# A fused conv/attention block: its first modulation moved to TensorE in four column groups, and a softmax scaling moved to GpSimd

## The chip, the core and the metric

The kernel runs on one core of a Trainium2 chip. A core has five engines that run side by side and wait for each other through semaphores: TensorE (PE in the profile; PEld is its weight load) does matmuls from SBUF into PSUM, VectorE (DVE), ScalarE (ACT) and GpSimd (POOL) work element by element, and SyncE (SP) here only issues DMAs. ACT issues some small DMAs too. The metric is the device time of one execution in microseconds (us); less is better.

## The reference

Two layers work on 256 latent tokens and 256 context tokens of width 1,024, in float32. Before any layer a vector `c` (and `c_ctx` for the context) gives nine modulation vectors per layer, three for each of three sublayers:

```python
mod = (jax.nn.silu(c) @ mod_w[i] + mod_b[i])          # 9 x 1024 per layer
h   = rms_norm(t, norm_g) * (1 + scale) + shift       # before each sublayer
t   = t + gate * sublayer(h)
```

The sublayers of layer 0 are a SwiGLU feed-forward network, a short convolution and another SwiGLU; those of layer 1 are a SwiGLU, an attention with 8 query heads and 2 key heads over all 512 tokens, and a SwiGLU. Only the latent tokens are the output. What matters here: nothing can be multiplied before the first shift (`B00` in the kernel) and scale (`A00`) are known, since the very first feed-forward product takes the modulated, normalised `x` of both streams.

## The kernel before

Activations are kept transposed: a tile has 128 of the 1,024 features on its partitions and 512 tokens (two streams `s` of 256) in its free dimension, so `x` is 8 tiles (`k`). To keep float32 accuracy with faster matmuls, `split` (L91) cuts every operand into a high part (ACT, L92, names ending in h) and a low part (DVE, L93, names ending in l), and `mm3` (L112) does three matmuls, wh*mh, wh*ml, wl*mh (lines L116, L117, L118). Raw weights arrive in a ring of three 1 MB buffers `wr` (L87), issued in order on SP (L88); a buffer is free again when its last reader is through.

Modulation is computed in one of two ways. A *unit* (L136, `junk`) is one DVE instruction that multiplies 1,024 columns of transposed weights with the broadcast `silu(c)` in `scbc` and sums them; `tick` sprinkles such units over the whole kernel, and `mod_ready` forces those that are due. For the first shift and scale, which everything waits for, there is `mod_pe` (L736): eight TensorE matmuls of 128x2 by 128x256 accumulate a row pair in PSUM, ACT copies it (L746), and two matmuls against `ident` turn it into columns (L748), which DVE adds to the bias (L753).

The start is written as a list of steps, issued in the program in this order:

```python
FIRST_STEPS = (
    "W0 P11 P10 P00 N0 P01 N1 P12 W1 S M00 M10 M01 M11 D02 N2 M02 D13 W2 D03 M12 M20 M21 N3 "
    "M03 M22 M13 M23"
)
```

The first digit of P and D is 0 for the shift and 1 for the scale, the last digit is the quarter `q` of the features (two `k` tiles). P is `mod_pe`, D is `mod_dve` (the same by four DVE units), N normalises and modulates a quarter (`norm_q` with `norm_k`: per tile and stream a DVE product `t`, L250, an ACT sum `hh`, L260, a DVE difference `hl`, L261, and an ACT copy for later, L265), W loads and splits one of the first three feed-forward tiles, M multiplies tile `i` with quarter `q` (12 matmuls into the PSUM pair `pg`, `pu`), and S loads and activates `scbc`. Ahead of the list, 36 matmuls of ones (L719) keep TensorE busy, and the root mean squares of both streams are found (`ss`). The list gives the program order; a planner in the framework then sets each engine's final order by priority and by when it expects operands, so an engine's instructions may stand in another order than the list. It does so for TensorE too.

All six large PSUM buffers belong to the three M tiles, so the following tile, and the stage `w13` of five more such tiles behind it, starts when the first of them is through.

In the attention, `scores` (L1022) makes for each head and each of two query halves a score tile `psc` of 128x512 on TensorE, its maximum on DVE (L1031), a negated scaled maximum (L1033), the exponential `e` with its sum on ACT (L1039), the sum's reciprocal `r` (DVE, L1043) and the scaled `pn` (DVE, L1047). `turn` (L1051) transposes `pn` on TensorE (L1056) and splits it (`pth` on ACT, `ptl` on DVE), and `mix` multiplies with the values. Scores run two heads ahead of `turn`; each head has a `tick(2)`, two more DVE units.

Of the kernel before, what the change touches and what calls it, by code (L numbers as in the profile page):

```python
# [9 lines left out]
F32 = mybir.dt.float32  # L10
F32R = mybir.dt.float32r
BF16 = mybir.dt.bfloat16
AF = mybir.ActivationFunctionType
ALU = mybir.AluOpType
AX = mybir.AxisListType

P = 128
D = 1024
KT = D // P
S = 256  # L20
# [6 lines left out]
KVH = 2  # L27
EPS = 1e-6
WARM = 36

FIRST_STEPS = (
    "W0 P11 P10 P00 N0 P01 N1 P12 W1 S M00 M10 M01 M11 D02 N2 M02 D13 W2 D03 M12 M20 M21 N3 "
    "M03 M22 M13 M23"
)


# [1 line left out]
def hybrid_kernel(ctx: ExitStack, tc: tile.TileContext, a: dict, out: bass.AP):  # L40
    nc = tc.nc
    const = ctx.enter_context(tc.tile_pool(name="const", bufs=1))
# [27 lines left out]
    ccol = cload("ccol", [P, KT, 2])  # L70
# [5 lines left out]
    ident = cload("ident", [P, P])  # L76
    ones = const.tile([P, P], F32, name="ones", tag="ones")
    nc.vector.memset(ones, 1.0)
    eps_t = const.tile([P, 1], F32, name="eps_t", tag="eps_t")
    nc.vector.memset(eps_t, EPS)  # L80
    sccol = const.tile([P, KT, 2], F32, name="sccol", tag="sccol")
    nc.scalar.activation(out=sccol, in_=ccol, func=AF.Silu)
    scbc = mp.tile([P, 2, D], F32, name="scbc", tag="scbc", bufs=1)


# [35 lines left out]
    modv = {}  # L121
# [29 lines left out]
    def mod_job(l, ch, pair):  # L151
        mod_tile(l, ch)
        raw = load_raw(a["modT"][l, ch * 4 + pair])
        for j in range(2):
            for v in range(streams(l, ch)):
                mod_unit(l, ch, pair, raw, j, v)
# [557 lines left out]
    h32 = {}  # L714
    idle = psmall("idle")


    for _ in range(WARM):
        nc.tensor.matmul(idle[:, :P], ones, ones, start=True, stop=True)  # L719
    for k in range(KT):  # L720
        square_add(k, 0, T2)
    ris = []
    for s in range(2):
        ris.append(tp.tile([P, S], F32, name=nm("ris"), tag=f"ris{s}", bufs=1))
        nc.scalar.copy(ris[s], rms_inv(s, (accs[s], accs[s, "last"])))
    A00 = const.tile([P, KT, 2], F32, name="A00", tag="A00")
# [3 lines left out]
        out=sb1, in0=modb[:, 0, KT : 2 * KT], scalar1=1.0, scalar2=None, op0=ALU.add  # L730
    )

    def both(t):
        return t.unsqueeze(2).to_broadcast([P, 2, 2])

    def mod_pe(ch, q):  # L736

        raw = load_raw(a["mod0"][ch, q])
        pr = psmall("pr")
        for k in range(KT):  # L740
            nc.tensor.matmul(
                pr[:2, :S], sccol[:, k, :], raw[:, k * S : k * S + S],
                start=(k == 0), stop=(k == KT - 1),
            )
        row = tp.tile([P, S], F32, name=nm("row"), tag="t", bufs=3)
        nc.scalar.copy(row[:2, :], pr[:2, :S])  # L746
        for j in range(2):
            nc.tensor.matmul(  # L748
                pr[:, S + 2 * j : S + 2 * j + 2], row[:2, j * P : j * P + P], ident[:2, :2],
                start=True, stop=True,  # L750
            )
        k2 = slice(2 * q, 2 * q + 2)
        nc.vector.tensor_tensor(  # L753
            out=(A00 if ch else B00)[:, k2, :],
            in0=pr[:, S : S + 4].rearrange("p (k v) -> p k v", v=2),
            in1=both(sb1[:, k2] if ch else modb[:, 0, k2]),
            op=ALU.add,
        )
# [11 lines left out]

    pps = [(psum("pg"), psum("pu")) for _ in range(3)]

    def mod_dve(ch, q):
        mod_job(0, ch, q)
        if ch:
            k2 = slice(2 * q, 2 * q + 2)
            nc.vector.tensor_scalar(
                out=A00[:, k2, :], in0=modv[0, 1][:, k2, :], scalar1=1.0, scalar2=None,
                op0=ALU.add,
            )  # L780

    ws, gs0 = {}, []

    def load_sc():
# [4 lines left out]
    def first_w(i):  # L789
# [8 lines left out]

    steps = {
        "P": mod_pe,  # L800
        "D": mod_dve,
        "S": load_sc,
        "W": first_w,
        "N": norm_q,
        "M": lambda i, q: w13_mm(pps[i], ws[i], h, range(2 * q, 2 * q + 2), 0, T2),
    }
    for step in FIRST_STEPS.split():
        steps[step[0]](*(int(c) for c in step[1:]))
    done[0, 0] = done[0, 1] = 16
    h = FirstBlocks(h, h32)  # L810
    for i in range(3):
# [15 lines left out]
    for m in range(KT):  # L827
# [4 lines left out]
        for c0, c1 in ((0, S), (S, T2)) if m == 0 else ((0, T2),):  # L832
# [13 lines left out]
        d = tp.tile([P, T2], F32, name=nm("d"), tag="gm", bufs=3)  # L846
        nc.vector.tensor_scalar(
            out=d, in0=u, scalar1=convk[:, 1, m : m + 1], scalar2=None, op0=ALU.mult
# [4 lines left out]
            out=d2[:, :, 1:], in0=u2[:, :, : S - 1], scalar=convk[:, 0, m : m + 1],  # L853
# [3 lines left out]
            out=d2[:, :, : S - 1], in0=u2[:, :, 1:], scalar=convk[:, 2, m : m + 1],  # L857
# [164 lines left out]
    def scores(hd):  # L1022
        kv = hd // (HEADS // KVH)
        r_ = []
        for qt in range(2):
            o = (hd % 2) * S + qt * P
            ps = psum("psc")
            mm3(ps, tuple(t[:, o : o + P] for t in qs[hd // 2]), ks[kv], True, True)
            ci = hd * 2 + qt
            mx = ap.tile([P, 1], F32, name=nm("mx"), tag="mx", bufs=4)  # L1030
            nc.vector.reduce_max(mx, ps, axis=AX.X)  # L1031
            nb = ap.tile([P, 1], F32, name=nm("nb"), tag="nb", bufs=4)
            nc.vector.tensor_scalar(  # L1033
                out=nb, in0=mx, scalar1=scq[:, ci : ci + 1], scalar2=-1.0,
                op0=ALU.mult, op1=ALU.mult,
            )
            e = tp.tile([P, T2], F32, name=nm("e"), tag="sg", bufs=3)
            sm = ap.tile([P, 1], F32, name=nm("sm"), tag="smx", bufs=4)
            nc.scalar.activation(  # L1039
                out=e, in_=ps, func=AF.Exp, scale=scq[:, ci : ci + 1], bias=nb, accum_out=sm  # L1040
            )
            r = ap.tile([P, 1], F32, name=nm("r"), tag="r", bufs=4)
            nc.vector.reciprocal(r, sm)  # L1043
            if qt == 0:
                pn2 = hot("pn", F32)
            pn = pn2[:, qt * T2 : qt * T2 + T2]
            nc.vector.tensor_scalar(out=pn, in0=e, scalar1=r, scalar2=None, op0=ALU.mult)  # L1047
            r_.append(pn)
        return r_

# [54 lines left out]
def _layout(inp):  # L1105
    f = lambda k: np.asarray(inp[k])
    d = {}

    def kp(w, width):

        k, n = w.shape
        v = w.reshape(k // P, P, n // width, width).transpose(2, 1, 0, 3)
        return v.reshape(n // width, P, (k // P) * width)

    tok = np.concatenate([f("x")[0], f("ctx")[0]], axis=0)
    d["xT"] = tok.T.reshape(KT, P, T2).transpose(1, 0, 2)
    d["c2"] = np.stack([f("c")[0], f("c_ctx")], axis=0)
    d["ccol"] = d["c2"].reshape(2, KT, P).transpose(2, 1, 0)
    mw = f("mod_w")
    m0 = mw[0][:, : 2 * D].reshape(KT, P, 2, 4, S)  # L1120
    d["mod0"] = m0.transpose(2, 3, 1, 0, 4).reshape(2, 4, P, 2048)
    d["modT"] = mw.transpose(0, 2, 1).reshape(2, 36, 2, P, D).transpose(0, 1, 3, 2, 4).reshape(2, 36, P, 2048)
    d["modb"] = f("mod_b").reshape(2, 72, P).transpose(2, 0, 1)
    d["normg"] = f("norm_g").reshape(2, 3, KT, P).transpose(3, 0, 1, 2)
    w13 = f("ffn_w13").reshape(2, 2, KT, P, 2, NM, P)[:, :, :, :, ::-1]
    d["w13"] = w13.transpose(0, 1, 5, 3, 4, 2, 6).reshape(2, 2, NM, P, 2048)
    w2 = f("ffn_w2").reshape(2, 2, NM, P, KT // 2, 2, P)
    w2 = w2.transpose(0, 1, 4, 3, 5, 2, 6)
# [12 lines left out]
    d["cw_b"] = kp(ci[:, :D], 256)  # L1141
    d["cw_out"] = kp(f("conv_w_out")[0], 256)
    d["convk"] = f("conv_k")[0].reshape(3, KT, P).transpose(2, 0, 1)
    wqkv = f("attn_w_qkv")[0]
    d["wq"] = kp(wqkv[:, :D], 256)
    d["wk"] = kp(wqkv[:, D : D + 256], 256)[0]
    d["wv"] = kp(wqkv[:, D + 256 :], 256)[0]
    d["wo"] = kp(f("attn_w_o")[0], 256)
    d["qg"] = f("attn_q_g")[0].reshape(P, 1)
    d["kg"] = f("attn_k_g")[0].reshape(P, 1)  # L1150


    pos = np.arange(S)
    inv = np.float32(10000.0) ** (-np.arange(32, dtype=np.float32) / np.float32(32))
    ar = (pos // 64).astype(np.float32)[:, None] * inv
    ac = (pos % 64).astype(np.float32)[:, None] * inv
    ang = np.concatenate([ar, ar, ac, ac], axis=-1).astype(np.float32)
    d["cosT"] = np.cos(ang).T
    sign = np.where(np.arange(P) % 64 < 32, -1.0, 1.0).astype(np.float32)
    d["sinT"] = np.sin(ang).T * sign[:, None]  # L1160
    d["ident"] = np.eye(P, dtype=np.float32)
    return {k: np.ascontiguousarray(v) for k, v in d.items()}


# [17 lines left out]
```

## Time and profile before

| what | value |
|---|---|
| median of three runs | 1605.62 us (1602.84 to 1607.07) |
| the profiled execution's own time | 1606.83 us |
| its span in the profile | 1605.0 us |
| TensorE clock granted, mean | 0.991 |
| first weight product of the first feed-forward network | 38.50 us after the start |
| mod0 loads (P) on SP | 5 of 1,024 KB, 7.6 us from issue to landing in the middle |
| DVE units of modulation (L136) | 236, 1,279 ns each |
| softmax scalings (L1047) | 16 on DVE |

A busy TensorE in the profile is not a TensorE at its best: a matmul with two useful columns counts as busy in the same way as one with 128. So the start is read from the names of the instructions, and the attention from what TensorE waits for.

### The profile page before, as it was taken

What the parts mean: (1) busy time and instruction counts of PE and PEld (TensorE: products, weight loads), DVE (VectorE), ACT (ScalarE), POOL (GpSimd) and SP (SyncE); (2) the same over time, 40 slices, a digit from 0 to 9 for tenths busy, and PEclk for the clock granted to TensorE, in tenths of its full rate; (3) what the DMA queues carried; (4) which work ended last, traced back from release to release, by engine and by line L of the source; (5) the groups of instructions that cost most, each with busy time, mean ns of one, the idle gap of its engine ahead of it and who ended that gap; (6) DMA issues with size and microseconds to landing.
All of it is one profiled execution on the core that took longest, in us unless ns stands there. A gap on an engine that the chain in (4) does not pass through costs nothing.

```text
span 1605.0 us, 25629 instructions
## 1 busy us (share of the span) xinstructions
PE 1578.0 (98%) x10590; PEld 1451.0 (90%) x10590; DVE 1322.5 (82%) x2021; ACT 717.7 (45%) x1100; POOL 0.2 (0%) x4
## 2 busy tenths in 40 slices
PE   9999999999999999999999999999999998899999
PEld 5788998998888899999899899889899897899999
DVE  4988788879998879799797998898797889965554
ACT  4632452544322366335255375245254455454443
POOL 0000000000000000000000000000000000000000
PEclk9999999999999999999999999999999999989999
DMA  8555334334565422452433423453433463755452
GB/s 299 184 184 184 105 101 175 105 117 159 183 223 196 158 79 90 148 184 99 153 130 122 170 78 117 159 184 99 164 120 112 165 217 107 280 191 186 169 197 106
DMA packets 38278, 248.79 MB, mean 155 GB/s; under 512 B 5136, under 2 KB 6928, under 8 KB 12304
## 3 DMA queue, kind: packets, MB, share of 16 engines
q1 hardware_dynamic: 35712, 245.38, 43.6%
q10 hardware_dynamic: 2448, 1.76, 0.4%
q8 instruction: 83, 1.36, 0.3%
q14 instruction: 35, 0.29, 0.1%
HBM read 244.77 MB, written 1.05 MB: 153 GB/s over the span
## 4 chain that ended last, share of the span: by engine, by line
PE 88%; DVE 8%; ACT 1%; DMA 1%; issue 1%; ACTq 0%; SPq 0%; DVEq 0%
PE py L117 9%; PE py L116 9%; PE py L118 9%; PE p L118 6%; PE p L117 6%; PE p L116 6%; PE q L118 5%; PE q L116 5%; PE q L117 5%; DVE junk L136 3%; PE pg L116 2%; PE pg L117 2%; PE pg L118 2%; PE pu L118 2%; PE pu L117 2%; PE pu L116 2%
## 5 line engine op out<-in xcount | busy, mean ns | idle before, releaser
L92 ACT ACTIVATE wh<-wr 128x1024 fp32r<-128x1024 f32 (+2 forms) x276 | 276.6, 1014 | 395.3 <-PE py L117 108.5
L93 DVE TENSOR_TENSOR wl<-wr,wh 128x1024 fp32r<-128x1024 f32 (+2 forms) x276 | 320.1, 1165 | 96.6 <-ACT wh L92 96.1
L136 DVE CUSTOM_DVE_ANT_0 junk<-wr,scbc,modb 128x1024 bf16<-128x1024 f32 x236 | 301.8, 1279 | 33.7 <-DMA wr<-in_modT 31.0
L116 PE MATMUL py<-gh,wh 128*128 128x512 f32 (+1 forms) x746 | 263.2, 353 | 0.0
L117 PE MATMUL py<-gl,wh 128*128 128x512 f32 (+1 forms) x746 | 263.1, 353 | 0.0
L118 PE MATMUL py<-gh,wl 128*128 128x512 f32 (+1 forms) x746 | 262.8, 352 | 0.0
L118 PEld LDWEIGHTS py<-gh,wl 128*128 128x128 f32 x746 | 141.1, 189 | 18.9
L116 PEld LDWEIGHTS py<-gh,wh 128*128 128x128 f32 x746 | 141.2, 189 | 18.6
L117 PEld LDWEIGHTS py<-gl,wh 128*128 128x128 f32 x746 | 141.2, 189 | 18.2
L93 DVE TENSOR_TENSOR wl<-ws,wh 128x1024 fp32r<-128x1024 f32 x108 | 131.7, 1223 | 29.0 <-ACT wh L92 28.9
L92 ACT ACTIVATE wh<-ws 128x1024 fp32r<-128x1024 f32 x108 | 113.5, 1058 | 68.7 <-PE p L117 35.5
L118 PE MATMUL p<-th,wl 128*128 128x256 f32 x432 | 122.3, 283 | 0.0
L117 PE MATMUL p<-tl,wh 128*128 128x256 f32 x432 | 122.2, 283 | 0.0
L116 PE MATMUL p<-th,wh 128*128 128x256 f32 x432 | 122.2, 283 | 0.0
L440 DVE SCALAR_TENSOR_TENSOR x<-py,G,x 128x256 f32<-128x256 f32 x168 | 73.9, 477 | 22.5 <-PE py L118 22.2
L116 PE MATMUL q<-bh,wh 128*128 128x256 f32 x320 | 90.6, 283 | 0.0
L117 PE MATMUL q<-bl,wh 128*128 128x256 f32 x320 | 90.6, 283 | 0.0
L118 PE MATMUL q<-bh,wl 128*128 128x256 f32 x320 | 90.6, 283 | 0.0
L116 PEld LDWEIGHTS p<-th,wh 128*128 128x128 f32 x432 | 82.9, 192 | 0.3
L117 PEld LDWEIGHTS p<-tl,wh 128*128 128x128 f32 x432 | 82.9, 192 | 0.3
L118 PEld LDWEIGHTS p<-th,wl 128*128 128x128 f32 x432 | 82.9, 192 | 0.0
L116 PE MATMUL pg<-hh,wh 128*128 128x256 f32 (+1 forms) x240 | 75.8, 316 | 4.0 <-ACT hh L260 4.0
(236 smaller groups left out, 4029.8 us busy)
## 6 DMA issues: line engine op xcount, KB each, us to landing
wr<-in_w SPq DMA_DIRECT2D x88, 1024.0 KB, 4.9
wr<-in_modT SPq DMA_DIRECT2D x67, 1024.0 KB, 4.9
wr<-in_w2b SPq DMA_DIRECT2D x32, 896.0 KB, 4.5
wr<-in_w2a SPq DMA_DIRECT2D x16, 1024.0 KB, 4.8
wr<-in_cw_cx SPq DMA_DIRECT2D x8, 1024.0 KB, 4.9
wr<-in_mod SPq DMA_DIRECT2D x5, 1024.0 KB, 7.6
wr<-in_cw_b SPq DMA_DIRECT2D x4, 1024.0 KB, 4.8
wr<-in_cw_out SPq DMA_DIRECT2D x4, 1024.0 KB, 4.8
```

The source lines that it names most:

```text
L92: nc.scalar.activation(out=hi, in_=src, func=AF.Copy)
L93: nc.vector.tensor_tensor(out=lo, in0=src, in1=hi.bitcast(F32), op=ALU.subtract)
L116: nc.tensor.matmul(ps, wh, mh, start=first, stop=False, **kw)
L117: nc.tensor.matmul(ps, wh, ml, start=False, stop=False, **kw)
L118: nc.tensor.matmul(ps, wl, mh, start=False, stop=last, **kw)
L136: nc.vector.tensor_tensor_reduce(out=junk, in0=raw[:, j * D : j * D + D], in1=scbc[:, v, :], scale=1.0, scalar=modb[:, l, col : col + 1], ...
L440: nc.vector.scalar_tensor_tensor(out=x[:, m, s * S : s * S + S], in0=ps[:, o : o + S], scalar=g[:, m, s : s + 1], in1=x[:, m, s * S : s * ...
```

## The change

- **The first modulation.** All eight quarters of shift and scale are now P steps; the D steps are gone. `sccol` is widened from 2 to 32 columns per tile, the rest zero. In a P step the eight matmuls are spread by `tile_position` over four groups of 32 columns of the array, two each, and so four partial sums land on four groups of 32 partitions in PSUM. ACT copies all 128 partitions, and the turn, a step of its own (T), multiplies with the new constant `rowsum`, which adds up the four groups while it turns.
- **The order.** The list begins with P10 and P00, has T steps, one F step (12 more matmuls of ones into `pps[2][0]`) and S at its end. `tc.manual_schedule` for TensorE makes that engine keep the order of the list; the other engines are still planned.
- **The softmax.** `pn = e * r` is issued on GpSimd instead of VectorE.

```diff
 FIRST_STEPS = (
-    "W0 P11 P10 P00 N0 P01 N1 P12 W1 S M00 M10 M01 M11 D02 N2 M02 D13 W2 D03 M12 M20 M21 N3 "
-    "M03 M22 M13 M23"
+    "P10 P00 T10 T00 F W0 N0 W1 M00 W2 M10 P11 M20 P01 T11 T01 N1 M01 P12 M11 P02 T12 T02 N2 "
+    "M21 P13 M02 P03 T13 T03 N3 M12 M22 M03 M13 M23 S"
 )
...
-    sccol = const.tile([P, KT, 2], F32, name="sccol", tag="sccol")
-    nc.scalar.activation(out=sccol, in_=ccol, func=AF.Silu)
+    sccol = const.tile([P, KT, 32], F32, name="sccol", tag="sccol")
+    nc.vector.memset(sccol, 0.0)
+    nc.scalar.activation(out=sccol[:, :, :2], in_=ccol, func=AF.Silu)
+
+    rowsum = cload("rowsum", [P, 2])
...
+    def fill(ps, n):
+
+        for _ in range(n):
+            nc.tensor.matmul(ps[:, :P], ones, ones, start=True, stop=True)
+
+    fill(idle, WARM)
...
         for k in range(KT):
+            g = 32 * (k % 4)
             nc.tensor.matmul(
-                pr[:2, :S], sccol[:, k, :], raw[:, k * S : k * S + S],
-                start=(k == 0), stop=(k == KT - 1),
+                pr[g : g + 32, :S], sccol[:, k, :], raw[:, k * S : k * S + S],
+                start=(k < 4), stop=(k >= 4), tile_position=(0, g),
             )
         row = tp.tile([P, S], F32, name=nm("row"), tag="t", bufs=3)
-        nc.scalar.copy(row[:2, :], pr[:2, :S])
+        nc.scalar.copy(row, pr[:, :S])
+        rows[ch, q] = pr, row
+
+    def mod_turn(ch, q):
+
+        pr, row = rows[ch, q]
         for j in range(2):
             nc.tensor.matmul(
-                pr[:, S + 2 * j : S + 2 * j + 2], row[:2, j * P : j * P + P], ident[:2, :2],
+                pr[:, S + 2 * j : S + 2 * j + 2], row[:, j * P : j * P + P], rowsum,
                 start=True, stop=True,
             )
...
-        "D": mod_dve,
+        "T": mod_turn,
+        "F": lambda: fill(pps[2][0], FILL),
...
-    for step in FIRST_STEPS.split():
-        steps[step[0]](*(int(c) for c in step[1:]))
+    with tc.manual_schedule(engines={mybir.EngineType.PE}):
+        for step in FIRST_STEPS.split():
+            steps[step[0]](*(int(c) for c in step[1:]))
...
-            nc.vector.tensor_scalar(out=pn, in0=e, scalar1=r, scalar2=None, op0=ALU.mult)
+            nc.gpsimd.tensor_scalar(out=pn, in0=e, scalar1=r, scalar2=None, op0=ALU.mult)
...
+    d["rowsum"] = (np.arange(P)[:, None] % 32 == np.arange(2)).astype(np.float32)
```

More of the change, by code (lines that the diff above doesn't have):

```diff
@@ L29 @@
 WARM = 36
+FILL = 12
 FIRST_STEPS = (
-    "W0 P11 P10 P00 N0 P01 N1 P12 W1 S M00 M10 M01 M11 D02 N2 M02 D13 W2 D03 M12 M20 M21 N3 "
-    "M03 M22 M13 M23"
+    "P10 P00 T10 T00 F W0 N0 W1 M00 W2 M10 P11 M20 P01 T11 T01 N1 M01 P12 M11 P02 T12 T02 N2 "
+    "M21 P13 M02 P03 T13 T03 N3 M12 M22 M03 M13 M23 S"
 )
@@ L715, in hybrid_kernel @@
     idle = psmall("idle")
-    for _ in range(WARM):
-        nc.tensor.matmul(idle[:, :P], ones, ones, start=True, stop=True)
+    def fill(ps, n):
+        for _ in range(n):
+            nc.tensor.matmul(ps[:, :P], ones, ones, start=True, stop=True)
+    fill(idle, WARM)
     for k in range(KT):
@@ L734, in both @@
         return t.unsqueeze(2).to_broadcast([P, 2, 2])
+    rows = {}
     def mod_pe(ch, q):
@@ L771, in hybrid_kernel @@
     pps = [(psum("pg"), psum("pu")) for _ in range(3)]
[L773 to L780, printed above, removed]
     ws, gs0 = {}, []
```

## The prediction

> **What bounds the kernel now.** I read the page's busy line, a table of ten-microsecond stretches, TensorE's instructions in order of time, the chain of waits, and then the stretch of the softmax.
>
> ```profile
> PE 1578.0 (98%) x10590; PEld 1451.0 (90%) x10590; DVE 1322.5 (82%) x2021; ACT 717.7 (45%) x1100; POOL 0.2 (0%) x4
> ```
>
> TensorE (PE) is the bound, and GpSimd (POOL) is free. Only time in which PE does no useful product can be won. The stretches (columns: stretch; length, then PE, PEld, DVE, ACT, POOL busy with counts; granted clock, DMA share, GB/s) show where that is at the start:
>
> ```profile
> 10.00:20.00 10.00, 8.49 (x45) 5.02 (x44) 3.94 (x9) 5.58 (x11) 0.00 (x0) 0.74 0.90 337
> 20.00:30.00 10.00, 10.00 (x46) 4.15 (x45) 1.53 (x6) 0.72 (x2) 0.00 (x0) 0.92 0.72 250
> 30.00:40.00 10.00, 10.00 (x49) 4.82 (x47) 7.01 (x17) 7.82 (x20) 0.00 (x0) 1.00 0.92 333
> 60.00:70.00 10.00, 7.23 (x33) 5.60 (x32) 10.00 (x22) 4.46 (x10) 0.00 (x0) 1.00 0.81 302
> ```
>
> PE looks full from 20 to 40 us, while DVE idles. TensorE's own instructions (start, duration) show with what:
>
> ```profile
> 15.75 7.38 PE L741 MATMUL pr<-wr,sccol 128*2 128x256 f32 x20 [1.03 <-DMA wr<-in_mod]
> ...
> 23.06 0.60 PE L748 MATMUL pr<-ident,row 2*128 2x2 f32 x4
> 23.59 3.62 PE L741 MATMUL pr<-wr,sccol 128*2 128x256 f32 x16
> ...
> 38.50 0.50 PE L116 MATMUL pg<-hh,wh 128*128 128x512 f32 x1
> ```
>
> That is the modulation: a P step takes 16 instructions of 0.2215 us (3.54 us) for two useful columns, a turn (T) 0.53 us, and the first weight product begins at 38.50. The chain then shows the other loss:
>
> ```profile
> 6.70 8.91 DMA wr<-in_mod
> ...
> 65.87 0.41 DVE t L250
> 66.30 0.52 ACT hh L260
> 66.86 0.50 PE pg L116
> ```
>
> DVE, full with three mod jobs (12 junk units of 1.20 to 1.27 us), brings the last normalised quarter so late that PE stands still for 2.9 us before 66.86. The 144 products of the first three w13 tiles (M) end at 75.35; the next 240 run without a gap to 129.75, 0.2267 us each. So M is 32.65 us of work, and 75.35 - 32.65 = 42.7 us of the start are not M.
>
> Around the softmax PE idles again (same columns):
>
> ```profile
> 1335.00:1370.00 35.00, 27.16 (x166) 22.16 (x165) 35.00 (x90) 20.58 (x48) 0.00 (x0) 0.95 0.34 121
> 1370.00:1415.00 45.00, 38.52 (x266) 36.54 (x266) 41.92 (x74) 21.91 (x36) 0.00 (x0) 0.85 0.72 261
> ```
>
> Here DVE is the bound: 35.00 of 35, while PE loses 7.84 us. Groups around it (ns min/median/max):
>
> ```profile
> L1039 ACT ACTIVATE e<-psc,nb,scq x16: 767/778/794, 1329.7 to 1362.8; 128x512 f32<-128x512 f32 x16
> L1047 DVE TENSOR_SCALAR pn<-e,r x16: 474/482/488, 1333.9 to 1366.2; 128x512 f32<-128x512 f32 x16
> ```
>
> and in the chain each of these scalings is one link:
>
> ```profile
> 1342.82 0.39 DVE pn L1047
> 1343.33 0.60 DVE mx L1031
> 1343.93 0.60 DVE ptl L93
> ```
>
> **Part 1, the start.** It takes away D02, D13 and D03 (12 x 1.27 = 15.2 us of DVE), adds three P and three T to PE, spreads a P over four groups of 32 columns, loads mod0 first, and fixes PE's order. I build the new order step by step; landings are those of the same places in the queue before.
>
> *Loads.* The three first transfers of a ring buffer landed at 12.7, 15.6 and 18.5, about 2.9 us apart. They are now P10, P00 and W0. Later ones wait for a buffer: W1 for P10, W2 for P00, P11 for W0's split, and so on, each 4.7 to 5.1 us from issue to landing. I get W1 22.5, W2 25.4, P11 28.3, P01 32.6, P12 34.8: each before PE reaches its step, so loads cost nothing; if one is late, the steps behind it on PE wait as long. Three modT loads become mod0 loads of the same 1,024 KB. The scbc loads (two issues on SP, 0.90 us) and their Silu (2.01 us and a table load of 1.28 on ACT) move behind P03; their first reader is a unit in the w13 stage after M, 20 us later, which covers them. The extra constant and the memset of sccol are under 0.2 us beside other work.
>
> *A P step.* The trace has no matmuls that run side by side. Below: four at once, 16 instructions in four slots, 0.89 us. Above: none, 3.54 us. A matmul here is two recorded instructions on one column group (80 records for 40 matmuls). If instructions start in order, the second half of one can share a slot with the first half of the next, on another group, and no more: 9 slots x 0.2215 = 2.0 us. I take 2.0, since M's records too start strictly one behind another.
>
> *PE's order.* The root-mean-square matmuls end at 14.7, as before. P10 and P00: 4.0 us at full clock. The clock was half from 14.8 to 21.7 after the lull before 15.75; now PE has work from 14.75 on, so I take half of that stretch (3.4 us, as the shortest in this trace) and end P00 at 20.4; with the whole stretch it is 2 us later. Row copy and hand-over 0.75 (22.30 to 23.06), T00 0.53, then twelve filling matmuls of 0.213, under which N0 runs (t 0.40, hh 0.51, hl 0.40 for two streams): M00 at 24.3 instead of 38.5. From there: M 32.65; six P 12.0; three pairs of T, 2 x 0.53 and 0.25 of waiting for the second copy, 3.9; M01 directly behind N1 waits 1.8, with P12 and all later steps behind it; a first product behind another shape took 0.50 against 0.39, so six returns 0.7. Sum 24.3 + 32.65 + 12.0 + 3.9 + 1.8 + 0.7 = 75.35. **That is zero gain**: the 14 us by which M starts earlier are spent on the P and T steps that now lie inside it. DVE's freed 15 us count only as the 2.9 us stall, already in this sum. Behind M the next tile's split needs W0's halves, free after M03, 5.5 us before M ends: 2.3 us of split, hidden.
>
> With P at 0.89 us, M00 is held by W0 (18.5 and 3 us of split) at 22.0: 22.0 + 32.65 + 5.3 + 3.9 + 1.8 + 0.7 = 66.4, a gain of 9.0. With 3.54, M00 is at 27.5 and the sum 87.8, a loss of 12.4.
>
> [...]
>
> **Part 2, the softmax.** 16 scalings leave DVE, where one is followed by the next instruction after 0.40 us: 6.4 us. DVE is full until about 1415, so this shortens the stretch nearly in full; PE has 7.8 us idle there to take it. The price on GpSimd isn't in the trace (its four memsets of one column say nothing): below 0.40, as on DVE; above 0.97, the Exp with its accumulator read (0.78 + 0.19), the slowest of this shape. I take 0.8, as ACT is the nearest separate engine. It hides because a head takes 4.0 us (1333.9 to 1366.2 over eight) and scores run two heads ahead. If DVE is no longer last, waits on ACT and PE come up: it idled 3.4 us in the 100 us shown, and I take off a third, 1.1. **Gain 5.3**; ends 0 and 9.8, the latter with 3.4 us if the half-clock stretch behind 1366 goes too.
>
> [...]
>
> **Sum.** The profiled execution took 1606.8 (span 1605.0), 1.2 above the median of 1605.6. 1606.8 - 0.0 - 5.3 = 1601.5, and by the median **1600.4**.
>
> **Rivals.**
> - *Four P matmuls at once*: 9.0 and 5.3, 1591.3. Against it: two instructions per matmul on one group.
> - *No overlap* (slower): the P steps take 3.54 and PE does three more than before, 12.4 - 5.3, 1612.7. Eight P steps make it slower from 2.7 us each (5.3 / 8 above my 2.0), by over 0.3% from 3.3. For it: no records of the profile show two matmuls side by side.
> - *GpSimd becomes the bound*: from 2.0 us per scaling, half a head. At 2.5 (0.97, a junk of 1.27 to wait behind, two hand-overs of 0.13) 16 x 0.5 = 8, 1613.
> - *The softmax gain doesn't arrive*, since hand-overs between DVE, GpSimd and PE replace it: 1605.7.
>
> **How the numbers follow.** What this kernel's runs can tell from no change is about 0.3%, 4.8 us. Likeliest 0.42, own range 1596 to 1605 (clock and softmax ends), faster 0.27, same 0.15. Four at once 0.20, all faster. No overlap 0.15, nearly all slower. GpSimd bound 0.10, 0.07 slower. No softmax gain 0.13: 0.02 faster, 0.09 same, 0.02 slower. Together 0.49 faster, 0.27 same, 0.24 slower. The range 1588 to 1613 reaches past the first two rivals.
>
> **What would show it.** Right: first pg matmul near 24, a P's eight matmuls in 2 us, M's 144th near 75, no junk before it, DVE below full between 1335 and 1370 and PE's idle there halved. Wrong: P at 0.9 or 3.5; pg waiting for W1 or W2's split or for a load; psc or pt waiting for pn on GpSimd; junk longer than 1.27 where pn runs.

## The result and the profile after

The changed kernel takes 1599.13 us (median of five runs, 1597.92 to 1601.16), the kernel before, run beside it, 1606.64 (1602.84 to 1607.07). The ratio is 0.9961, with a 95% interval from 0.9947 to 0.9975: 0.4% faster. The forecast was 1600.4. The profiled execution took 1601.16 us, its span 1599.4, against 1605.0 before.

The total is near what was forecast; the way to it, above all in the start, is not. First the page's busy line of the kernel after:

```profile
PE 1572.9 (98%) x10674; PEld 1452.2 (91%) x10674; DVE 1304.2 (82%) x1984; ACT 718.6 (45%) x1103; POOL 29.7 (2%) x20
```

TensorE loses 5.1 us of busy time, VectorE 18.3, and GpSimd has work. The stretches, in the same columns as before (stretch; length, then PE, PEld, DVE, ACT, POOL busy; granted clock, DMA share, GB/s), show the start and the softmax:

```profile
10.00:20.00 10.00, 10.00 (x102) 8.72 (x102) 4.23 (x16) 5.91 (x13) 0.00 (x0) 1.00 0.96 366
20.00:30.00 10.00, 7.40 (x30) 4.57 (x28) 9.17 (x17) 7.89 (x17) 0.00 (x0) 1.00 0.78 277
30.00:40.00 10.00, 7.51 (x52) 4.70 (x52) 1.95 (x7) 1.78 (x5) 0.00 (x0) 0.83 0.84 306
60.00:70.00 10.00, 10.00 (x46) 8.33 (x46) 9.53 (x19) 8.71 (x17) 0.00 (x0) 1.00 0.31 105
...
1335.00:1370.00 35.00, 28.35 (x181) 23.90 (x180) 32.42 (x80) 23.05 (x52) 26.48 (x15) 0.95 0.41 147
1370.00:1415.00 45.00, 39.85 (x294) 38.53 (x293) 39.92 (x69) 22.16 (x37) 0.00 (x0) 0.89 0.71 257
```

The stall between 60 and 70 us is gone. In its place TensorE idles 2.6 us from 20 to 30 and 2.5 from 30 to 40, where it had been full (with modulation), and the clock from 30 to 40 is 0.83. TensorE's instructions in order of time (start, duration; in brackets idle time ahead and its releaser) name the reasons:

```profile
14.76 1.93 PE L754 MATMUL pr<-wr,sccol 128*32 128x256 f32 x32
...
20.72 0.50 PE L122 MATMUL pg<-hh,wh 128*128 128x512 f32 x1
...
30.81 1.94 PE L754 MATMUL pr<-wr,sccol 128*32 128x256 f32 x16 [2.52 <-DMA wr<-in_mod]
36.11 1.07 PE L754 MATMUL pr<-wr,sccol 128*32 128x256 f32 x16
37.11 1.21 PE L766 MATMUL pr<-rowsum,row 128*128 128x2 f32 x8
40.32 0.63 PE L122 MATMUL pg<-hh,wh 128*128 128x512 f32 x1 [2.00 <-ACT hh L266]
```

A P step takes 1.0 us (two take 1.93), not 2.0: four column groups do run at the same time. The first weight product starts at 20.72 us instead of 38.50. Yet the 144th product of M ends at 74.04 against 75.35. Between the two, TensorE waits for P11's load (2.5 us) and for N1 (2.0), and from about the end of each wait the clock is granted at half for 3.4 us (30.3 to 33.7, 40.5 to 44.0): P11 takes 1.94 us there, a P step at full clock 1.07.

In the softmax, the groups by tile (ns min/median/max) and who waited:

```profile
L1058 POOL TENSOR_SCALAR pn<-e,r x16: 1559/1566/2635, 1332.0 to 1366.2; 128x512 f32<-128x512 f32 x16
...
  PEld pt L1067: 5.4, 5
  PE pt L1067: 3.0, 3
```

A scaling costs 1.56 us on GpSimd, up to 2.6, against 0.48 on VectorE, and TensorE's transposes wait 3.0 us for it. VectorE, 35.00 of 35 us busy before, is at 32.42.

To place the gain I use four points of TensorE's record: the end of M's 144th product, the first score product, the last transpose, and the first product of the statistics (`ss`) after the out projection. From scores to statistics the kernel before took 79.0 us (1323.6 to 1402.6), the kernel after 74.7 (1322.7 to 1397.4): 2.3 us of it up to the last attention product, 1.8 in the out projection, 0.2 between. Of the span's 5.6 us, 1.3 are therefore the start, 4.3 the softmax with what follows it, and the rest cancels. Not all of the 4.3 need be VectorE's time: of the stretches of half clock, 6.8 us lay in this part before (1366.5 to 1373.3) and 3.4 after (1341.0 to 1344.4), and a stretch costs TensorE half its length at most (in the one from 40.5 us on, M's products start 0.43 us apart, behind it 0.23).

### The profile page after: what moved, and what is told of

It is laid out like the page before. It is cut to its first block, busy times and chain, and to the rows that moved or that the text cites. A ratio compares the mean times of both kernels' runs of the same rounds, so it can differ in the third digit from the quotient of the medians.

```text
span 1599.4 us, 25805 instructions
## 1 busy us (share of the span) xinstructions
PE 1572.9 (98%) x10674; PEld 1452.2 (91%) x10674; DVE 1304.2 (82%) x1984; ACT 718.6 (45%) x1103; POOL 29.7 (2%) x20
## 4 chain that ended last, share of the span: by engine, by line
PE 87%; DVE 7%; DMA 3%; ACT 1%; issue 1%; POOL 0%; DVEq 0%; ACTq 0%; SPq 0%; POOLq 0%
PE py L122 8%; PE py L123 8%; PE py L124 8%; PE p L123 6%; PE p L122 6%; PE p L124 6%; PE q L124 5%; PE q L122 5%; PE q L123 5%; PE pg L122 3%; PE pg L123 3%; PE pg L124 3%; PE pu L124 3%; PE pu L123 3%; PE pu L122 3%; DVE junk L142 2%
## 5 line engine op out<-in xcount | busy, mean ns | idle before, releaser
L142 DVE CUSTOM_DVE_ANT_0 junk<-wr,scbc,modb 128x1024 bf16<-128x1024 f32 x224 | 287.0, 1281 | 38.9 <-DMA wr<-in_modT 36.3
```

Source lines behind the costliest of these rows:

```text
L142: nc.vector.tensor_tensor_reduce(out=junk, in0=raw[:, j * D : j * D + D], in1=scbc[:, v, :], scale=1.0, scalar=modb[:, l, col : col + 1], ...
```

## The experiments

All kernels, in one table. "M" is the end of the 144th product in the profile, "softmax" the time from scores to statistics, "half" half the length of all stretches of half clock within the span, which is what they cost a busy TensorE. Each ratio is to the kernel before of the same series; its medians were 1605.39 to 1607.33 from series to series, so medians of different rows are to be compared to some 2 us only.

| kernel | median us | ratio to before, 95% | M | softmax | half |
|---|---|---|---|---|---|
| before | 1606.64 | 1 | 75.35 | 79.0 | 13.7 |
| after | 1599.13 | 0.9961 [0.9947, 0.9975] | 74.04 | 74.7 | 11.9 |
| scaling only | 1600.03 | 0.9956 [0.9941, 0.9971] | 73.63 | 73.7 | 8.5 |
| start only | 1604.37 | 0.9985 [0.9974, 0.9995] | 70.71 | 79.5 | 12.0 |
| one group | 1618.55 | 1.0072 [1.0055, 1.0089] | 91.55 | 75.1 | 10.7 |
| two groups | 1606.61 (one run) | | 78.65 | 77.1 | 10.2 |
| M20 ahead of P11 | 1594.75 | 0.9923 [0.9906, 0.9939] | 69.23 | 74.7 | 8.9 |
| own buffers | 1593.23 | 0.9915 [0.9900, 0.9930] | 69.39 | 74.2 | 7.1 |
| no scaling | 1598.14 | 0.9945 [0.9928, 0.9962] | 72.32 | 73.1 | 10.6 |
| half on each | 1603.10 | 0.9978 [0.9967, 0.9988] | 71.21 | 78.2 | 13.7 |
| scaling on ScalarE | 1601.58 | 0.9963 [0.9950, 0.9977] | 72.30 | 78.9 | 15.4 |
| M20 split | 1594.95 | 0.9938 [0.9924, 0.9953] | 66.51 | 76.2 | 13.7 |
| gap filled, P12's tile | 1600.04 | 0.9970 [0.9959, 0.9981] | 72.40 | 74.2 | 10.5 |
| gap filled, P01's tile | 1596.79 | 0.9941 [0.9928, 0.9955] | 67.48 | 75.4 | 7.2 |

M, softmax and half come from one profiled execution of each kernel, and they vary where nothing was changed. The start of the kernel after stands in five of these profiles (after, start only, no scaling, half on each, scaling on ScalarE), and M ends at 70.7 to 74.0 in them, 72.1 in the mean; that of the kernel before in two, 73.6 and 75.4. The attention with all scalings on GpSimd stands in nine, with 73.7 to 77.1 us for the softmax, 75.0 in the mean; that with all on VectorE in two, 79.0 and 79.5. So the start is worth about 2.4 us and the softmax about 4.2, and a difference of 1 or 2 us between single profiles shows nothing.

My theory after the result: the scaling brings the gain, by VectorE's relief; the start earns its 18 us of earlier products (38.50 to 20.72) and gives them back to exposed waits. The rivals: the start brings it; or the side-by-side groups are worth nothing.

### One part at a time

The kernel before with the second part alone:

```diff
-            nc.vector.tensor_scalar(out=pn, in0=e, scalar1=r, scalar2=None, op0=ALU.mult)
+            nc.gpsimd.tensor_scalar(out=pn, in0=e, scalar1=r, scalar2=None, op0=ALU.mult)
```

> The kernel before with the softmax scaling alone moved to GpSimd. Theory: the two traces place about 4.3 us of the 5.6 us between the spans behind the start, so the span is near 1600.7 and the ratio near 0.997; GpSimd takes 1.56 us per scaling alone and 2.3 to 2.6 where a modulation unit runs on DVE beside it, and the unit keeps its 1.27 us. Rival (the gain is all in the start): 1605, ratio 1.000.

Measured: 1600.03 us, 7.1 below the kernel before of the same series (1607.11). The softmax shrinks by 5.3 us, from 79.0 to 73.7. The rest of the profile's gain is clock: M ends 1.7 us sooner though nothing there was changed, because this execution had one stretch of half clock of 3.4 us in the start, and that of before one of 6.8; near 1,400 us it is 6.8 against 10.2.

The kernel after with the scaling back on VectorE:

```diff
-            nc.gpsimd.tensor_scalar(out=pn, in0=e, scalar1=r, scalar2=None, op0=ALU.mult)
+            nc.vector.tensor_scalar(out=pn, in0=e, scalar1=r, scalar2=None, op0=ALU.mult)
```

> The changed kernel with the softmax scaling back on VectorE: the start alone. Theory: the first three tiles and the five behind them end at 128.4 instead of 129.7, 1.3 us, so the span is near 1603.7, ratio 0.999. Rival (the gain is all in the start): 1599.4, ratio 0.9965.

Measured: 1604.37 us, 2.7 below; the interval of the ratio, 0.9974 to 0.9995, allows 0.8 to 4.2. So most of the gain is the scaling's. The two parts alone give 0.44% and 0.15%, both at once 0.39%; the intervals are wide enough for the parts to add.

Its profile shows how much the start depends on one landing. TensorE's order of time again:

```profile
28.53 1.07 PE L754 MATMUL pr<-wr,sccol 128*32 128x256 f32 x16
32.49 1.07 PE L754 MATMUL pr<-wr,sccol 128*32 128x256 f32 x16
33.50 1.21 PE L766 MATMUL pr<-rowsum,row 128*128 128x2 f32 x8
36.71 0.50 PE L122 MATMUL pg<-hh,wh 128*128 128x512 f32 x1 [2.00 <-ACT hh L266]
```

Here P11 was issued at 23.2 us and landed at 28.16, and TensorE did not wait; in the kernel after, issued at 22.9, it landed at 30.67. A load lands in 16 pieces. In the kernel after, 15 of P11's had landed by 27.75 us, and one came at 30.67; here all came from 27.61 to 28.16. So one late piece of 16 made the difference. Without that wait and the half clock behind it, M ends at 70.71, 3.3 us sooner by the same list of steps. Of the five profiles with this list, TensorE waited for P11 in two, 2.5 us in the kernel after and 1.2 with the scaling on ScalarE. A last piece over 1 us behind the 15 others is seen in 8 to 14 of the some 230 loads into `wr` of every profile.

### What the column groups are worth

The kernel after with all eight K tiles of a P step in one group of 32 columns:

```diff
-            g = 32 * (k % 4)
             nc.tensor.matmul(
-                pr[g : g + 32, :S], sccol[:, k, :], raw[:, k * S : k * S + S],
-                start=(k < 4), stop=(k >= 4), tile_position=(0, g),
+                pr[:32, :S], sccol[:, k, :], raw[:, k * S : k * S + S],
+                start=(k == 0), stop=(k == KT - 1),
             )
```

> The changed kernel with the eight matmuls of a P step one behind another on one group of 32 columns (the turn then reads 32 partitions). Theory (side by side really saves 2.5 us per step): a P step takes 3.5 us instead of 1.0, eight of them 20 us; the 2.5 us for which P11 waits for its load and some of the half-clock stretches are used up, so the span grows by 12 to 20 us, to 1611 to 1619. Rival (the records only look overlapped, or P steps hide in waits): under 3 us more, up to 1602.

Measured: 1618.55 us. M ends at 91.55, 17.5 us later than in the kernel after, and the time is 19.4 higher. TensorE's record of one P step:

```profile
34.00 3.64 PE L753 MATMUL pr<-wr,sccol 128*32 128x256 f32 x16
```

And with two groups (`g = 32 * (k % 2)`, the first two tiles start, the last two stop, copies and sums over 64 rows):

> The kernel after with the K of the first modulation in two parts side by side on 32 columns each instead of four. One group alone took 3.64 us for the eight products of a P step, four groups 1.07. Theory (groups run at the same time, so the step goes by the products of one group): 4 products in a row, about 1.8 to 1.9 us, and the time of one look 1602 to 1607. Rival (the step's 1.07 us has another cause, the 128 columns in use): nearer 3.6 than 1.8.

Measured in one execution: 1606.61 us, and for a P step:

```profile
31.32 1.92 PE L754 MATMUL pr<-wr,sccol 128*32 128x256 f32 x16
```

3.64, 1.92 and 1.07 us for one, two and four groups: the step goes by the products of one group. The records show it as well: in the kernel after, the four instructions of a row start at 45.172, 45.179, 45.186 and 45.192 us, the next row at 45.412, then 0.216 us apart. So the rival "four at once" had the mechanism right, and without it the whole change would have been a loss.

### Filling the waits of the start

The kernel after with two steps moved: M20 ahead of P11, P12 ahead of M01.

```diff
-    "P10 P00 T10 T00 F W0 N0 W1 M00 W2 M10 P11 M20 P01 T11 T01 N1 M01 P12 M11 P02 T12 T02 N2 "
+    "P10 P00 T10 T00 F W0 N0 W1 M00 W2 M10 M20 P11 P01 T11 T01 N1 P12 M01 M11 P02 T12 T02 N2 "
```

> The changed kernel with two steps moved in the list: M20 ahead of P11, which waits for its load, and P12 ahead of M01, into the gap behind N1. Theory (TensorE's fixed order exposes waits that other work could fill): 2 to 2.5 us at P11, 1.0 at P12, and up to 3.4 if the half-clock stretches go, so the span is 1593 to 1597. Rival (the loads set the pace, since a ring buffer comes free late, so the wait only moves to P01): under 1.5 us, 1598 to 1600.

Measured: 1594.75 us, 4.4 below the kernel after, and the intervals of the two ratios don't meet. M ends at 69.23 in place of 74.04 (72.1 in the mean of the five profiles). The exposed waits are now 1.7 us before P01 and 0.3 before P12, since M20 covers P11's landing and P12 covers a part of N1:

```profile
30.46 1.07 PE L754 MATMUL pr<-wr,sccol 128*32 128x256 f32 x16
33.26 1.07 PE L754 MATMUL pr<-wr,sccol 128*32 128x256 f32 x16 [1.72 <-DMA wr<-in_mod]
34.26 1.20 PE L766 MATMUL pr<-rowsum,row 128*128 128x2 f32 x8
35.73 1.68 PE L754 MATMUL pr<-wr,sccol 128*32 128x256 f32 x16 [0.27 <-DMA wr<-in_mod]
```

The time given back in the start was in the order of the steps, not in their cost.

Then the question whether the ring of load buffers or the memory sets when P11 and P01 land. The modulation blocks of quarters 1 to 3 get buffers of their own and are issued ahead of need (a new step L, its place on SP written out too):

```diff
+    def loads(*qs):
+        for q in qs:
+            for ch in (1, 0):
+                own[ch, q] = [hot("pw", F32) for _ in range(2)]
+                for i in range(2):
+                    nc.sync.dma_start(
+                        own[ch, q][i], a["mod0"][ch, q][:, i * 1024 : i * 1024 + 1024]
+                    )
...
-    "P10 P00 T10 T00 F W0 N0 W1 M00 W2 M10 P11 M20 P01 T11 T01 N1 M01 P12 M11 P02 T12 T02 N2 "
-    "M21 P13 M02 P03 T13 T03 N3 M12 M22 M03 M13 M23 S"
+    "P10 P00 T10 T00 F W0 N0 W1 M00 W2 L12 M10 P11 M20 P01 T11 T01 N1 P12 M01 P02 L3 M11 T12 T02 N2 "
+    "M21 P13 P03 M02 T13 T03 N3 M12 M22 M03 M13 M23 S"
```

> The kernel after, but the raw modulation blocks of quarters 1 to 3 are loaded into buffers of their own ahead of need, and no longer wait for DVE to free the ring that W0, W1 and W2 fill; P12 stands ahead of M01, as in the order of the run before. Theory (the ring sets the pace of the first 75 us: P11's load was issued at 22.9 us, when W0's split had freed a buffer, and landed at 30.7, where TensorE waited 2.5 us): no TensorE wait on a modulation load is left, the 144th product of M ends near 67 us against 74.0 in the kernel after and 69.2 with M20 ahead of P11, and the time is near 1593 us. Rival (the memory sets it: 18 to 36 us moved 330 to 425 GB/s with the DMA engines 0.8 to 1.0 busy, so an earlier load only makes its neighbour late): W1 or W2 lands later instead, the 144th product ends at 69 us or later, and the time is 1595 us or more.

Measured: 1593.23 us, the lowest median of all. M ends at 69.39, not at 67, as the rival said, but not for its reason: W1 and W2 land no later than in the kernel after (22.16 and 24.64, against 23.15 and 25.63). From 27 us on a block of 512 KB lands every 1.28 us, without a pause, and P01 is complete at 31.0 instead of 33.6. TensorE waits for no load any more, as the theory said, only for N1:

```profile
34.93 1.07 PE L767 MATMUL pr<-pw,sccol 128*32 128x256 f32 x16
37.81 0.78 PE L122 MATMUL pg<-hh,wh 128*128 128x512 f32 x1 [1.81 <-ACT hh L266]
```

The 1.5 us to the kernel with M20 ahead are not in the start; the profiled executions differ by 1.8 us of half clock. That the buffers themselves earn anything is not shown.

### Is the half clock caused by the waits?

Nearly every stretch of half clock in the starts of these profiles begins during a stand of TensorE of 1 to 3 us, or up to 3 us behind one; not every stand has one (the same lull near 15 us has it in the kernel before, and not with the scaling alone; the stall of 2.8 us before 66.86 has none in the kernel before, and the same one has it with the scaling alone). Nor does the length of a stand set that of the stretch: behind or in the same 2.0 us before M01 it is 3.4 us in two profiles and 6.8 in three. Two edits take the 1.81 us stand away, both on the kernel with own buffers. The first puts half of M20 into it:

```diff
-    "P10 P00 T10 T00 F W0 N0 W1 M00 W2 L12 M10 P11 M20 P01 T11 T01 N1 P12 M01 P02 L3 M11 T12 T02 N2 "
+    "P10 P00 T10 T00 F W0 N0 W1 M00 W2 L12 M10 P11 H200 P01 T11 T01 N1 H201 P12 M01 P02 L3 M11 T12 T02 N2 "
...
+        "H": lambda i, q, k: w13_mm(pps[i], ws[i], h, range(2 * q + k, 2 * q + k + 1), 0, T2),
```

> The kernel with the modulation blocks in buffers of their own, but M20 (four k of... two input blocks of the third pair of weight columns) is cut in two: its first block stays between P11 and P01, its second goes behind T01, where TensorE stood 1.81 us for ScalarE's first hh of N1 and the clock was granted at half for 3.4 us right after. Theory (the stand and the half clock behind it are one loss, of 1.8 + 1.7 us, and independent products placed there take both away): no gap over 0.5 us between 24 and 45 us, no half-clock stretch before 75, the 144th product at 65.5 to 66.5 us in place of 69.4, the time near 1590. Rival (memory sets it, the blocks land 1.28 us apart without a pause: P01 is now wanted 1.4 us earlier than it was and TensorE stands there instead): the 144th product at 68 us or later, the time 1592 or more.

Measured: the start as the theory had it. M ends at 66.51, there is no half clock before 75 us (three stretches of the start, same columns as above):

```profile
24.00:36.00 12.00, 11.86 (x86) 7.35 (x85) 7.53 (x17) 6.97 (x16) 0.00 (x0) 1.00 1.01 397
36.00:48.00 12.00, 11.79 (x77) 8.39 (x80) 5.98 (x16) 4.94 (x13) 0.00 (x0) 1.00 1.03 418
48.00:75.00 27.00, 27.00 (x139) 22.09 (x132) 24.21 (x41) 18.84 (x33) 0.00 (x0) 1.00 0.24 81
```

But the median is 1594.95, no better. The six executions spread from 1591.60 to 1598.33, with a mean granted clock of 0.996 to 0.991; executions with 0.991 and 0.996 lie up to 6.7 us apart. The profiled one, the longest, has half clock at 570, 1052 and 1267 us, where the kernel with own buffers has none.

The second edit puts products of ones there, which do nothing:

```diff
-... T11 T01 N1 P12 M01 ...
+... T11 T01 N1 P12 G M01 ...
...
+        "G": lambda: fill(rows[1, 2][0], 6),
```

> The kernel with the modulation blocks in buffers of their own, with 6 products of ones by ones (12 records, 0.112 us each: 1.3 us) behind P12, where TensorE stood 1.81 us before M01. They compute nothing that is used; the wait for hh stays. Theory (the half-clock stretches of the start follow a stand of TensorE): the stretch of 3.4 us behind this gap goes, M's first product of quarter 1 still starts near 37.8 us, the 144th ends near 67.7 in place of 69.4, and the time is 1591.5, 1.7 below. Rival (the stretches come by another count, not by this gap): there is still one of 3.4 us before 75 us and the time stays at 1593.2 or goes up by the few tenths that the fill is too long.

Measured: 1600.04 us, a failure of the edit. The filling wrote P12's PSUM tile and so had to wait for ScalarE's copy of P12, which stands in ScalarE's queue behind N1's work; TensorE's record and the waits:

```profile
38.76 2.93 PE L726 MATMUL pr<-ones 128*128 128x128 f32 x12 [2.79 <-ACT row L772]
```

The stand grew to 2.8 us, and the half clock that began in it lasted 6.8. Into P01's tile instead, which had been read:

```diff
-        "G": lambda: fill(rows[1, 2][0], 6),
+        "G": lambda: fill(rows[0, 1][0], 7),
```

> The filling of the gap once more, now into the PSUM tile of P01, which ScalarE and DVE have read by then: in the run before, the filling products wrote P12's tile and so waited 2.79 us for ScalarE's copy of P12, which stood behind N1's hh; the gap grew and the half clock behind it lasted 6.9 us. Here 7 products of ones (14 records, 1.6 us) fall into the 1.81 us before M01. Theory (half clock follows a stand of TensorE): TensorE stands 0.5 us at most between 24 and 45 us, no half-clock stretch before 75 us, the 144th product ends near 67.7 (69.4 without the filling). Rival: a stretch of 3.4 us is there all the same, and the 144th ends at 69 or later. Of the time: 1591.5 if the clock of the rest is that of the kernel without the filling; up to 1595 if stretches come later instead, as after the split of M20, where three of them lay between 570 and 1270 us.

```profile
34.25 1.07 PE L767 MATMUL pr<-pw,sccol 128*32 128x256 f32 x16
35.25 1.83 PE L726 MATMUL pr<-ones 128*128 128x128 f32 x14
37.13 0.50 PE L122 MATMUL pg<-hh,wh 128*128 128x512 f32 x1
```

M ends at 67.48 (67.7 expected), and there is no half clock before 75 us. Useless products took the half clock away, so in the start it does go with the stand: of the 13 stands of 1.7 us or more between 24 and 70 us in these profiles, 12 have half clock in or behind them, and the two profiles without such a stand have none. Each of these is one execution. The time is 1596.79 all the same, and the executions spread from 1594.23 (clock 0.995) to 1599.89 (0.991). What the start saves is not found again in the median: the mean clock of these executions is 0.991 to 0.996, against 0.995 to 0.996 with own buffers alone, so half clock must lie elsewhere in some of them. Why is open, and the three kernels ran in three different series; no run here tells whether an unbroken start is the cause.

### What is left in the softmax

The kernel after without the multiplication at all (the exponential writes `pn`):

```diff
-            nc.gpsimd.tensor_scalar(out=pn, in0=e, scalar1=r, scalar2=None, op0=ALU.mult)
...
-                out=e, in_=ps, func=AF.Exp, scale=scq[:, ci : ci + 1], bias=nb, accum_out=sm
+                out=pn, in_=ps, func=AF.Exp, scale=scq[:, ci : ci + 1], bias=nb, accum_out=sm
```

> The kernel after with the softmax scaling left out altogether: ScalarE's exponential writes pn itself and nothing is multiplied by 1/sum, so the attention is unscaled. It bounds what is left in the scaling's place. From the first score product to the first output of the statistics after the out projection the kernel before took 79.0 us and the kernel after 74.7. Theory (with the scaling gone from DVE, GpSimd's 1.56 to 2.6 us is the next wait in the chain: 5.6 us of the chain in that stretch are pn's): the stretch takes 71 to 73 us and the time is 1595 to 1597. Rival (DVE, 42.1 of 46.0 us busy there, sets it still, and the waits for pn are filled by others when they go): the stretch stays within 0.7 us of 74.7, the time within 1.5 of 1599.

Measured: 1598.14 us, 1.0 below the kernel after; 73.1 us from scores to statistics, 1.6 less. The rival's bounds hold for the time, and neither theory's for the stretch. The intervals of the two ratios overlap, the stretch is only 0.5 us below the lowest of the nine profiles with GpSimd, and there is no half clock before the out projection here, where the kernel after has 3.4 us; so what GpSimd's slow scaling still costs can't be told from nothing. The transposes end 4.3 us sooner after the first (29.2 us instead of 33.5), but the out projection takes 28.2 instead of 25.5 and gives 2.7 back. The chain there has the load of its last weights:

```profile
1379.39 7.14 DMA wr<-in_wo
```

In the kernel after this load took 4.7 us. 15 of the 16 pieces landed within 5.4 us here too, and the last one late. It takes 7.8 and 7.3 us in two profiles with the scaling on GpSimd (two groups, gap filled by P01's tile), so the long out projection needn't come from the faster softmax. Nor is VectorE free: it is 48.98 of the 50 us from 1320 to 1370 busy, against 46.06 in the kernel after. Which of the two would hold a faster softmax back is open.

Half of the scalings on each engine:

```diff
-            nc.gpsimd.tensor_scalar(out=pn, in0=e, scalar1=r, scalar2=None, op0=ALU.mult)
+            (nc.gpsimd if qt == 0 else nc.vector).tensor_scalar(out=pn, in0=e, scalar1=r, scalar2=None, op0=ALU.mult)
```

> The kernel after with the second of each pair of scalings back on DVE: 8 on GpSimd, 8 on DVE at 0.48 us. Theory (it is DVE's time that was worth something: 16 x 0.48 = 7.7 us less gave 4.3 to 5.3 us from scores to statistics): half of it comes back, the stretch takes 76.5 to 77.5 us and the time is 1601 to 1602. Rival (GpSimd's latency is the larger cost by now: two scalings in a row take 3.1 us and more on GpSimd, 2.0 with the second on DVE): the stretch takes 73 us or less and the time is 1598 or less.

Measured: 1603.10 us, 4.0 above the kernel after, and 78.2 us in the softmax. The rival, 73 us or less, is out. The theory's half would be 77.1 between the means of 75.0 and 79.2; that 78.2 is more than half lost isn't shown, with profiles of one attention up to 3.4 us apart. The groups of `pn`:

```profile
L1058 POOL TENSOR_SCALAR pn<-e,r x8: 1562/2550/2644, 1330.8 to 1363.8; 128x512 f32<-128x512 f32 x8
L1058 DVE TENSOR_SCALAR pn<-e,r x8: 476/521/909, 1331.8 to 1366.1; 128x512 f32<-128x512 f32 x8
```

The median on GpSimd is 2.55 us where it was 1.57, and six of its eight now start while a modulation unit runs on VectorE; two of the eight on VectorE, both beside one on GpSimd, took 0.91 and 0.84 instead of 0.48 (five others beside one took 0.48 to 0.52). GpSimd's latency was not the larger cost; VectorE's time was.

All of them on ScalarE (`nc.scalar.activation(out=pn, in_=e, func=AF.Identity, scale=r)` in place of the GpSimd line):

> The kernel after with the scaling on ScalarE (identity with a scale by row) in place of GpSimd. ScalarE was 26.9 of 46.0 us busy in the stretch of the softmax; the nearest rows are its copies of 128x512, 0.6 us, so 16 more are 9.6 us: 36.5 of 46. Theory (DVE's relief is what counts, and who takes the scaling matters only by its latency): 0.6 us in place of 1.56 to 2.6 makes the stretch from scores to statistics 73 to 74 us, the time 1597 to 1599. Rival (ScalarE, which also makes every exponential and every high part, becomes the chain): the stretch takes 76 us or more, the time is 1601 or more.

Measured: 1601.58 us and 78.9 us, in the rival's bounds. But the profiled execution, 1605.09 us, is the longest of six, and the ratio, 0.9963, can't be told from the 0.9961 of the kernel after; so the profile speaks for the rival, and the time doesn't settle it. Each takes 0.72 us, less than half of GpSimd's, but ScalarE is 38.50 of the 50 us from 1320 to 1370 busy and makes every exponential. What TensorE waits for in the attention is now about half its results, half VectorE's:

```profile
PE pav L122 <- ACT e L1050: 2.3, 1, 2.3
PE pav L122 <- DVE ptl L99: 2.2, 2, 1.5
PE pt L1067 <- ACT e L1050: 1.7, 2, 1.0
```

By this profile GpSimd is a right place not for its speed but because nothing else waits in its queue: in the kernel after, the 16 scalings are all it does in those 50 us, 29.52 of them.

## Why the prediction was right, and where it was not

*The total.* 1600.4 was forecast from a start of no gain and a softmax gain of 5.3; 1599.13 came, from 1.3 and 4.3 in the profile, or by medians 2.7 and 7.1 with each part alone. The bounds of the softmax term, 0 and 9.8, held it. The start came out near zero from a sum in which several terms were wrong in opposite directions: that part of the hit is luck. (Two sums are off in the last digit: 1605.6 - 5.3 is 1600.3, and the rival of GpSimd as the bound, 1605.6 + 8, is 1613.6.)

*A P step, 2.0 us.* It took 1.00. The failed step is the inference that, since a matmul is two recorded instructions on one group and M's records start strictly one behind another, a group's second half could share a slot only with its neighbour's first half. The records of the change start four at a time. M's products each use all 128 columns; that their records come one behind another said nothing on groups. From one group to four the step goes from 3.64 to 1.07 us, 3.4 times. Going from M's shape to P's and back costs little here: from the last M record to the first P record 0.32 us, from the last P record to the next M 0.31, against 0.23 from product to product, 0.2 us for a step with both changes.

*The start's sum.* With a P step of 0.89 the prediction gave 66.4 and a gain of 9.0; the real end was 74.04. The 7.6 us between are: P11 waited for, 2.5; two stretches of half clock, 3.4; P steps of 1.0 instead of 0.89, 0.6; 1.1 us inside M00 and M10, which waited for W0's low half and for N0; 0.4 more at N1; less 1.3, since M00 began at 20.7 instead of 22.0. That is 6.7; 0.9 is left over and not assigned.

*"Each before PE reaches its step, so loads cost nothing".* This is the term that failed in the profiled execution. The landings were right to 0.7 us for W1 and W2 (23.15, 25.63), 2.4 late for P11 (30.67 against 28.3), 1.0 and 1.3 for P01 and P12. And since a P step takes 1.0 us, TensorE comes for P11 at 28.3 and not at some 29.7 (24.3 and two steps of M at 2.72): of the 2.5 us of waiting, 1.4 are its own earlier arrival and the rest the late landing. The same saving that shortens the steps uncovers the loads. The prediction named the price ("if one is late, the steps behind it on PE wait as long") and then didn't apply it to its own faster case. It is not the term that failed every time: of the five profiles with this list, three have no wait for P11. What all five have is the stand of 2.0 us for N1, for which the sum had 1.8, and 3.4 or 6.8 us of half clock in or behind the stands, for which it had nothing there.

*The half clock.* 3.4 us of it were taken near 15 to 20 us, where there was none (clock 1.00 from 10 to 30). It came with the new waits instead, 6.8 us in two stretches: beside the 2.5 and 2.0 us of the waits, up to 3.4 us more of a busy TensorE.

*A scaling, 0.8 us.* It took 1.56, and 2.3 to 2.6 in five of sixteen cases. ScalarE was the wrong neighbour to take it from; the value lies between the 0.97 of the upper bound and the 2.0 from which GpSimd would be the bound, a little too near the latter: a head is 4.0 us and two scalings are 3.1 to 4.2. The kernel without the scaling puts what it still cost at 1.0 us, not clear of the noise.

*The relief.* "DVE below full" was right (32.42 of 35). "PE's idle there halved" was wrong: 7.84 became 6.65. 1.8 of the 4.3 us arrive one stage later, in the out projection: the second load of its weights is issued at 1364.86 us instead of 1375.96, and TensorE's waits there for `wh` and `wl` fell from 2.0 to 1.0 us. The half clock behind 1366, which the upper end counted with 3.4 us, did go; another stretch of 3.4 us came at 1341.

*VectorE beside GpSimd.* "Junk longer than 1.27 where pn runs" was named as a sign of failure. No unit beside a scaling is longer (1.27 to 1.29 us); the scalings that start within one are (2.3 to 2.6 us against 1.56). A unit that starts up to 0.46 us before the recorded end of a scaling lengthens neither, and with half of the scalings on each engine one starts 0.96 us before it, with 1.26 us for the unit and 1.56 for the scaling. What makes the others longer no run here shows.

## What to carry to other kernels

When a step on the critical engine becomes faster, recompute the arrival at every later wait with the faster step before calling a load hidden; the order of the steps, at no cost, then decides what remains (here 4.4 us). Work moved off a full engine can go where nothing else queues, even at three times its duration (1.56 us against 0.48); judge it by the engine it leaves, and look for its gain also one stage behind the place of the edit. And before a difference of 1 or 2 us in one profile is given a cause, look how far the same stretch varies in profiles of kernels that don't change it: here a late piece of a load and a stretch of half clock did as much.

## What the hardware showed unexpectedly

- **Column groups.** Eight float32 products of 32 columns by 256 take 3.64, 1.92 and 1.07 us in one, two and four groups; four records start within 20 ns.
- **GpSimd beside a VectorE unit.** A scaling that starts while a modulation unit runs on VectorE takes nearly as much longer as the unit still runs (0.1 us less in the five cases). One case, VectorE's order of time and the scaling's group above: the scaling starts at 1338.12 us and takes 2.64, the unit runs from 1338.04 to 1339.31; 1.27 of the unit less the 0.08 that had passed, and 1.56, are 2.75, against 2.64.

```profile
1338.04 1.27 DVE L142 CUSTOM_DVE_ANT_0 junk<-wr,scbc,modb 128x1024 bf16<-128x1024 f32 x1
```

- **Half clock from short stands.** Stands of 1.7 to 2.8 us in the start came with 3.4 or 6.8 us at half clock in 12 of 13 cases, and there was none in the two profiles where products filled the stand.
- **One late piece of a load.** A 1 MB load lands in 16 pieces; in 8 to 14 of some 230 loads of a profile the last is over 1 us behind the others (P11: 2.9 us), at changing places.
- **One program, many clocks.** The same kernel (M20 split) was granted 0.991 to 0.996 from one execution to the next, with times up to 6.7 us apart, about as much as the larger part of this change; two starts that were 2 and 3 us shorter in the profile didn't show in a median.
